# A half-rotary embedding on one core: where the first load is cut, when the second store is issued, and which queue carries the third

## The chip, the core and the metric

The kernel runs on one core of one Trainium2 chip. The metric is the device time of one execution in microseconds (us), as the median over several executions. The profile page belongs to one further execution taken with the hardware profiler; its span runs from the first to the last recorded instruction of the core.

## The reference

The input `x` is float32 with the shape (16, 512, 16, 64): batch, position, head, element. Only the first 32 elements of a head are rotated, the first 16 of them against the second 16, by the angle tables `cos` and `sin` of the position; the last 32 elements are passed through unchanged.

```python
x1, x2 = x[..., :32], x[..., 32:]
rotated_first  = x1[..., :16] * cos[..., :16] - x1[..., 16:] * sin[..., :16]
rotated_second = x1[..., :16] * sin[..., :16] + x1[..., 16:] * cos[..., :16]
return np.concatenate([rotated_first, rotated_second, x2], axis=-1)
```

All of `x` has to be read and all of the output written: 33.55 MB each way.

## The kernel before

The positions are cut into four tiles, t = 0 to 3. A tile puts 16 consecutive positions ("rows", `K = 16`) on each of the 128 partitions; a row is 16 heads of 64 elements, 4 KB, so that a tile is 64 KB per partition and 8.39 MB in all. Three tiles fit on the chip at a time: `ring` has three slots (`NS = 3`), and tile t lies in slot t mod 3. Tile 3 therefore goes into the slot of tile 0 and cannot be loaded before tile 0 has been stored.

Everything is done in place in the ring. `load(t, lo, hi)` (L55) brings rows lo to hi of a tile, `store(t)` (L58) sends a whole tile out, passed-through elements included. Both are issued from the SP queue, which issues in program order and stops at the first transfer whose condition does not yet hold. One transfer reads or writes one contiguous run per partition, 4 KB times its number of rows. Only the two small table loads (L63, L64, 64 KB each) go through GpSimd's queue (POOL).

VectorE (DVE) first clears a staging tile (L61), spreads the two tables over all partitions when they have arrived (L73, L80, L83), and then does the arithmetic. `rotate(t, lo, hi)` handles rows lo to hi with four instructions: L96 multiplies by the sine table into `b_t` (a single buffer in PSUM), L97 multiplies by the cosine table in place, and L98 and L101 subtract and add `b_t`. A tile is rotated in two halves of 8 rows (`KC = 8`), and `turn(t)` is the two halves and the store.

The order on SP is that of the program: load 0, load 1, the first half of load 2; store 0, which waits for the arithmetic of tile 0; the second half of load 2; load 3 in two pieces of 14 rows and 2 rows (`KL = 14`), which wait until store 0 has landed; then stores 1, 2 and 3. Store 1 carries one dependence written by hand: besides its arithmetic it waits until the piece of 14 rows of load 3 (`near`) has landed.

Of the kernel before, what the change touches and what calls it, by code (L numbers as in the profile page):

```python
# [1 line left out]

# [4 lines left out]


@with_exitstack
def kernel(  # L10
    ctx: ExitStack,
    tc: tile.TileContext,
    x: bass.AP,
    cos: bass.AP,
    sin: bass.AP,
    out: bass.AP,
):
    nc = tc.nc
    fp32 = mybir.dt.float32
    P = 128  # L20
    B, S, H, D = x.shape
    Q = D // 4
    HF = D // 2

    K = 16
    T = B * S // (P * K)
    PB = S // K
    REP = P // PB  # L30
    R = H * D
    NS = 3
    KC = K // 2
    KL = 14

    xf = x.rearrange("b s h d -> (b s h d)").rearrange("(t p f) -> t p f", t=T, p=P)
    of = out.rearrange("b s h d -> (b s h d)").rearrange("(t p f) -> t p f", t=T, p=P)
    cosf = cos.rearrange("(p k) j -> p (k j)", k=K)
    sinf = sin.rearrange("(p k) j -> p (k j)", k=K)

    const_pool = ctx.enter_context(tc.tile_pool(name="const", bufs=1))
    b_pool = ctx.enter_context(tc.tile_pool(name="bp", bufs=1, space=bass.MemoryType.PSUM))


    ring = const_pool.tile([P, NS, K, H, D], fp32)
    stage = const_pool.tile([P, 2, K, HF], fp32)
    spun = const_pool.tile([P, 2 * K, Q], fp32)
    packed = const_pool.tile([PB, 2 * K, Q], fp32)
    table = const_pool.tile([P, 2, K, 2, Q], fp32)

    def rows(t, lo, hi):
        return ring[:, t % NS, lo:hi].rearrange("p k h d -> p (k h d)")

    def load(t, lo=0, hi=K):
        return nc.sync.dma_start(out=rows(t, lo, hi), in_=xf[t, :, lo * R : hi * R])  # L55

    def store(t, lo=0, hi=K):
        return nc.sync.dma_start(out=of[t, :, lo * R : hi * R], in_=rows(t, lo, hi))  # L58


    nc.vector.memset(stage[:, :, :, 0:Q], 0.0)  # L61
    spread = stage.rearrange("(j b) t k i -> j b t (k i)", b=REP)
    nc.gpsimd.dma_start(out=spread[:, 0, 0], in_=cosf)  # L63
    nc.gpsimd.dma_start(out=spread[:, 0, 1], in_=sinf)  # L64
    load(0)
    load(1)
    load(2, 0, KC)

    PQ = PB // REP
    nc.vector.stream_shuffle(  # L73
        out=spun[:],
        in_=stage.rearrange("p t k j -> p (t k) j")[:, :, 0:Q],
        mask=[j % PQ * REP for j in range(PB)],
    )
    for q in reversed(range(REP)):
        n = PQ * (q + 1)
        nc.vector.tensor_copy(out=packed[0:n], in_=spun[q * PB : q * PB + n])  # L80

    for r in range(REP):
        nc.vector.tensor_copy(  # L83
            out=table[r * PB : (r + 1) * PB].rearrange("p t k c j -> p (t k) c j"),
            in_=packed.unsqueeze(2).to_broadcast((PB, 2 * K, 2, Q)),
        )
    C = table[:, 0].rearrange("p k c j -> p k (c j)")
    Sn = table[:, 1].rearrange("p k c j -> p k (c j)")

    def rotate(t, lo, hi):  # L90
        x1 = ring[:, t % NS, lo:hi, :, 0:HF]
        c = C[:, lo:hi].unsqueeze(2).to_broadcast((P, hi - lo, H, HF))
        s = Sn[:, lo:hi].unsqueeze(2).to_broadcast((P, hi - lo, H, HF))
        b_full = b_pool.tile([P, KC, H, HF], fp32, name="b_t")
        b_t = b_full[:, 0 : hi - lo]
        nc.vector.tensor_mul(out=b_t, in0=x1, in1=s)  # L96
        nc.vector.tensor_mul(out=x1, in0=x1, in1=c)  # L97
        nc.vector.tensor_sub(  # L98
            out=x1[:, :, :, 0:Q], in0=x1[:, :, :, 0:Q], in1=b_t[:, :, :, Q:HF]
        )  # L100
        nc.vector.tensor_add(  # L101
            out=x1[:, :, :, Q:HF], in0=x1[:, :, :, Q:HF], in1=b_t[:, :, :, 0:Q]
        )

    def turn(t):
        rotate(t, 0, KC)
        rotate(t, KC, K)
        return store(t)

    turn(0)  # L110
    load(2, KC, K)
    near = load(3, 0, KL)
    load(3, KL, K)

    tc.add_manual_dep(
        turn(1).ins,
        near.ins.name,
        mybir.DependencyInfo(mybir.DependencyClass.Sync, mybir.DependencyReason.DATA),
        reason="the store follows the loads at the DMA engines",
    )  # L120
    turn(2)
    turn(3)


# [1 line left out]
_INS = ['x', 'cos', 'sin']  # L126
_OUTS = [((16, 512, 16, 64), 'float32')]


# [23 lines left out]
```

## Time and profile before

| what | before |
|---|---|
| median of 8 executions | 161.54 us (161.46 to 161.68) |
| profiled execution, its own time | 161.5 us |
| profiled execution, span | 159.7 us |
| DVE busy | 112.4 us, 70% of the span |
| POOL busy | 1.4 us |
| moved by DMA | 67.24 MB, 421 GB/s over the span |

The profiled execution's own time is 1.8 us longer than its span, and it lies within 0.04 us of the median. A DMA is listed where it was issued; its "us to landing" is the time from there to the last of its bytes. Transfers issued by one queue land one after the other here, so the time between two landings says how long the later one took. The DMA share is that of the 16 DMA engines together; in short windows it can exceed 1 or fall to 0, because a packet is counted whole where it begins.

### The profile page before, as it was taken

Reading aid. Unit: us, or ns where it says so; the run is one execution under the profiler, and the core shown is the slowest. Engines: PE = TensorE matmul, PEld = TensorE weight load, DVE = VectorE, ACT = ScalarE, POOL = GpSimd, SP = SyncE. Lnnn points to the kernel's source line nnn. Section 1 sums busy time; section 2 is a strip of 40 time slices with the busy share of each in tenths; the row PEclk is TensorE's granted clock in tenths of the full one; section 3 lists DMA queues with packets and bytes.
Section 4 is the critical chain, followed back from the end, with each engine's and each line's share of the span. In section 5 each row is a group of like instructions: output and inputs, shape, how many; then the busy total and the mean of one; then the engine's idle time right before and its main releaser. Section 6 shows DMA issues by size and latency. Waiting matters only on the chain.

```text
span 159.7 us, 113 instructions
## 1 busy us (share of the span) xinstructions
DVE 112.4 (70%) x43; POOL 1.4 (1%) x6
## 2 busy tenths in 40 slices
DVE  1000959999999999999999999999999960000000
POOL 3000000000000000000000000000000000000000
DMA  7969989999799699699999995996996996996992
GB/s 263 542 263 542 427 361 525 394 394 525 304 476 533 295 492 525 279 377 451 468 460 460 460 460 244 544 525 263 525 525 263 525 525 263 525 509 279 525 427 98
DMA packets 1504, 67.24 MB, mean 421 GB/s; under 512 B 192, under 2 KB 192, under 8 KB 224
## 3 DMA queue, kind: packets, MB, share of 16 engines
q1 hardware_dynamic: 1440, 67.11, 97.7%
q0 software_dynamic: 64, 0.13, 0.2%
HBM read 33.69 MB, written 33.55 MB: 421 GB/s over the span
## 4 chain that ended last, share of the span: by engine, by line
DVE 59%; DMA 14%; issue 7%; DVEq 1%
DVE b_t L96 22%; DVE ring L97 22%; DMA ring<-in_x_dram 14%; DVE ring L101 10%; DVE ring L98 4%; DVEq L148 1%; DVEq L96 0%
## 5 line engine op out<-in xcount | busy, mean ns | idle before, releaser
L96 DVE TENSOR_TENSOR b_t<-ring,table 128x4096 f32<-128x4096 f32 x8 | 35.5, 4432 | 2.1 <-DMA ring<-in_x_dram 1.9
L97 DVE TENSOR_TENSOR ring<-ring,table 128x4096 f32<-128x4096 f32 x8 | 35.4, 4424 | 0.3
L98 DVE TENSOR_TENSOR ring<-ring,b_t 128x2048 f32<-128x2048 f32 x8 | 18.3, 2287 | 0.3
L101 DVE TENSOR_TENSOR ring<-ring,b_t 128x2048 f32<-128x2048 f32 x8 | 18.2, 2280 | 0.0
L73 DVE LOAD_MASK_SELECT spun<-stage x1 | 0.0, 14 | 14.4 <-DMA stage<-in_sin_dram 14.4
L83 DVE COPY table<-packed 32x1024 f32<-32x1024 f32 x4 | 2.7, 684 | 0.1
L80 DVE COPY packed<-spun 32x512 f32<-32x512 f32 (+3 forms) x4 | 1.7, 416 | 0.1
L61 DVE MEMSET stage<- 128x512 f32 x1 | 0.5, 485 | 0.9 <-PEq L137 0.9
L73 DVE STREAM_SHUFFLE spun<-stage 128x512 f32<-128x512 f32 x1 | 0.7, 723 | 0.0
L63 POOL DMA_DIRECT2D stage<-in_cos_dram x1 | 0.6, 649 | 1.3 <-DVE stage L61 1.3
L64 POOL DMA_DIRECT2D stage<-in_sin_dram x1 | 0.5, 532 | 0.0
L137 POOL MEMSET const-float32-0.0<- 128x1 f32 x1 | 0.1, 93 | 0.2 <-issue 0.2
L137 POOL MEMSET const-bfloat16-1.0<- 128x1 bf16 x1 | 0.1, 95 | 0.0
L137 POOL MEMSET const-float32-1.0<- 128x1 f32 x1 | 0.1, 93 | 0.0
L137 POOL MEMSET const-uint8-127<- 128x1 uint8 x1 | 0.1, 92 | 0.0
## 6 DMA issues: line engine op xcount, KB each, us to landing
ring<-in_x_dram SPq DMA_DIRECT2D x2, 4096.0 KB, 40.7
ring<-in_x_dram SPq DMA_DIRECT2D x1, 7168.0 KB, 26.6
ring<-in_x_dram SPq DMA_DIRECT2D x1, 1024.0 KB, 28.7
stage<-in_cos_dram POOLq DMA_DIRECT2D x1, 64.0 KB, 9.0
stage<-in_sin_dram POOLq DMA_DIRECT2D x1, 64.0 KB, 13.3
out_dram<-ring SPq DMA_DIRECT2D x4, 24.9
ring<-in_x_dram SPq DMA_DIRECT2D x2, 31.7
```

The lines of the kernel that those rows point to most:

```text
L61: nc.vector.memset(stage[:, :, :, 0:Q], 0.0)
L63: nc.gpsimd.dma_start(out=spread[:, 0, 0], in_=cosf)
L64: nc.gpsimd.dma_start(out=spread[:, 0, 1], in_=sinf)
L73: nc.vector.stream_shuffle(out=spun[:], in_=stage.rearrange("p t k j -> p (t k) j")[:, :, 0:Q], mask=[j % PQ * REP for j in range(PB)],)
L80: nc.vector.tensor_copy(out=packed[0:n], in_=spun[q * PB : q * PB + n])
L83: nc.vector.tensor_copy(out=table[r * PB : (r + 1) * PB].rearrange("p t k c j -> p (t k) c j"), in_=packed.unsqueeze(2).to_broadcast((PB, ...
L96: nc.vector.tensor_mul(out=b_t, in0=x1, in1=s)
L97: nc.vector.tensor_mul(out=x1, in0=x1, in1=c)
L98: nc.vector.tensor_sub(out=x1[:, :, :, 0:Q], in0=x1[:, :, :, 0:Q], in1=b_t[:, :, :, Q:HF])
L101: nc.vector.tensor_add(out=x1[:, :, :, Q:HF], in0=x1[:, :, :, Q:HF], in1=b_t[:, :, :, 0:Q])
L137: nc = _bacc.Bacc("TRN2", target_bir_lowering=False, num_devices=1)
L148: with _tile.TileContext(nc) as tc:
```

## The change

Four things are changed. Load 0 becomes two transfers of 4 and 12 rows. Load 3 becomes one transfer of 16 rows. The arithmetic of the second half of tile 2 is cut into 5 rows and 3 rows (`KM = 13`), and store 1 waits for the last instruction on the 5 rows instead of a landing of load 3. Store 2 is issued from GpSimd's queue instead of SP's. `turn` is written out in full; `rotate` returns its last instruction so that store 1 can name it.

```diff
-    KL = 14
+    KM = 13
...
-    def store(t, lo=0, hi=K):
-        return nc.sync.dma_start(out=of[t, :, lo * R : hi * R], in_=rows(t, lo, hi))
+    def store(t, lo=0, hi=K, queue=nc.sync):
+        return queue.dma_start(out=of[t, :, lo * R : hi * R], in_=rows(t, lo, hi))
...
-    load(0)
+    load(0, 0, KC // 2)
+    load(0, KC // 2, K)
     load(1)
     load(2, 0, KC)
...
-        nc.vector.tensor_add(
+        return nc.vector.tensor_add(
             out=x1[:, :, :, Q:HF], in0=x1[:, :, :, Q:HF], in1=b_t[:, :, :, 0:Q]
         )
...
-    def turn(t):
-        rotate(t, 0, KC)
-        rotate(t, KC, K)
-        return store(t)
-
-    turn(0)
+    rotate(0, 0, KC)
+    rotate(0, KC, K)
+    store(0)
     load(2, KC, K)
-    near = load(3, 0, KL)
-    load(3, KL, K)
+    load(3)
+    rotate(1, 0, KC)
+    rotate(1, KC, K)
+    behind_loads = store(1)
+    rotate(2, 0, KC)
+    near = rotate(2, KC, KM)
+    rotate(2, KM, K)
+    store(2, queue=nc.gpsimd)
 
     tc.add_manual_dep(
-        turn(1).ins,
+        behind_loads.ins,
         near.ins.name,
         mybir.DependencyInfo(mybir.DependencyClass.Sync, mybir.DependencyReason.DATA),
         reason="the store follows the loads at the DMA engines",
     )
-    turn(2)
-    turn(3)
+    rotate(3, 0, KC)
+    rotate(3, KC, K)
+    store(3)
```

## The prediction

> **What bounds the kernel now.** I read the page first: how busy the engines are, and what the DMA queues moved.
>
> ```profile
> DVE 112.4 (70%) x43; POOL 1.4 (1%) x6
> ...
> q1 hardware_dynamic: 1440, 67.11, 97.7%
> q0 software_dynamic: 64, 0.13, 0.2%
> HBM read 33.69 MB, written 33.55 MB: 421 GB/s over the span
> ```
>
> No compute engine is near full. The packets of q1 (the SP queue) hold the 16 DMA engines 97.7% of the span, so the first suspicion is that the kernel is a pipe that is already full. Section 4 of the page seems to say otherwise, with DVE on 59% of the chain that ended last. In order of time, that chain ends so:
>
> ```profile
> 121.61 4.43 DVE ring L97
> 126.05 0.02 issue
> 126.07 2.29 DVE ring L98
> 128.36 2.20 DVEq L148
> ```
>
> It stops at 130.56, 29 us before the end of the span, and leaves out the last two stores. So I rebuilt the landings by hand from the trace, one answer per window around each issue: issue time plus "us to landing". The SP lines of the timeline give the issues, these two the end of it:
>
> ```profile
> 98.38 0.34 SPq L58 DMA_DIRECT2D out_dram<-ring  x1
> ...
> 103.69 0.34 SPq L58 DMA_DIRECT2D out_dram<-ring  x1
> ...
> 130.58 0.33 SPq L58 DMA_DIRECT2D out_dram<-ring  x1
> ```
>
> Load 0 lands at 22.9, load 1 at 42.3, half of load 2 at 52.0, store 0 at 71.7, the other half at 81.4, load 3 at 98.3 and 100.8, store 1 at 98.38 + 21.7 = 120.1, store 2 at 103.69 + 35.7 = 139.4, store 3 at 130.58 + 28.1 = 158.7. A tile takes 19.3 us in every one of these steps (8.39 MB / 19.3 us = 435 GB/s), whether load or store, with two exceptions: load 0 needs 22.2 us from its issue, and store 0 19.7. Each transfer is issued before its forerunner has landed: stores 0, 1, 2, 3 by 2.1, 2.4, 16.4 and 8.8 us. DVE, too, is kept waiting by data only at the start:
>
> ```profile
> DVE spun L73 <- DMA stage<-in_sin_dram: 14.4, 1, 14.4
> DVE b_t L96 <- DMA ring<-in_x_dram: 1.9, 1, 1.9
> ```
>
> Eight tiles' worth at 19.3 us are 154.4 us of the 159.7. Of the remaining 5.3, load 0 holds 22.2 - 19.3 = 2.9, its issue at 0.74, the teardown after the last landing 1.0, store 0 some 0.4, small change the rest. **The DMA engines are the bound from about 2 us to 158.7 us**, and an edit counts only if it changes the bytes, opens a hole in that stream, or changes the rate.
>
> **What the Trainium skill says.** (1) "DMA: Bandwidth & Descriptors", section "Issuing engines are not separate DMA queues": transfers from SP and GpSimd run on the same 16 DMA engines and interleave. The trace agrees: the tables on q0 land at 10.7 and 15.7, among SP's packets, though 64 KB each. (2) The same page, "SWDGE vs HWDGE vs iDMA": on GpSimd's queue software writes the descriptors, and packets are preferably at most 4096 B. The DMA summary counts 32 packets between 2 and 8 KB, which for 0.13 MB is 4 KB each: two 2 KB rows put together. Whether a 64 KB row stays whole there, the trace before does not show. (3) "SBUF — State Buffer", "Who interferes with whom": `tensor_tensor` has no 2-port mode; with both inputs in SBUF it contends with GpSimd's reads only, and that descriptor writing escapes it is called inferred. Not shown here either: POOL issues at 1.70 and 2.35, when DVE is idle. (4) "VectorE: DVE Perf Modes", "The TRN2 errata", gives (N + 151) / 0.96 ns for an fp32 `tensor_tensor`: 4424 ns for 4096 elements, and L97's row has 4424. I use its slope below.
>
> **The change part by part.**
>
> *Load 0 in two.* One more SP issue, 0.42 us (median of L55's first three), ahead of load 1. Covered: load 0's bytes keep the engines busy to 22.9, and load 1 is then issued near 1.6 instead of 1.2. Each partition has one more run here and one fewer in load 3 (joined into one), ten transfers of 128 runs before and after: the per-run and per-completion costs cancel. The join also makes SP issue once at 71.7 instead of twice (0.81 us for both): hidden, as the second half of load 2 fills the engines to 81.4. DVE does not start earlier: rows 0 to 8 touch both pieces, so L96 still waits for the second to land, near 22.9. The shorter first runs let the table packets of q0 in sooner, so `sin` may land some us before 15.7; table work (15.81 to 21.18) then ends earlier, but already ended 1.9 us before load 0. Worth nothing. What I can't price is the slow start: of the 2.9 us extra, about 1.0 is from issue to the first packet (DMA is first busy near 1.7), 0.3 the tables' bytes (q0 has 1.3% of the first 25 us), the rest the first fill and the completion. Shorter first runs could save half of that 1.6, or cost a little: -0.8 to +0.2; I take 0, since a first fill is a wait for the first bytes, which the length of the run does not shorten.
>
> *DVE, tile 2's second half in 5 and 3 rows.* Eight rows are 12,288 elements in four instructions and step 13.44 us (76.81 to 90.25), of which 12,288 / 0.96 = 12.80 us streams and 0.64 is fixed. Five rows: 8.00 + 0.64 = 8.64; three rows: 4.80 + 0.64 = 5.44. So `near` ends at 90.25 + 8.64 = 98.9, tile 2 at 104.3 instead of 103.7, tile 3 at 131.2 instead of 130.6. The cost is 0.64 us on DVE, hidden: the engines hold stores 1 and 2 until 139.4, so store 3 at 131.2 still comes 8.2 us early. With that cover gone it would cost 0.64.
>
> *Store 1 at a point of DVE's work.* Issue moves from 98.4 to 98.9; the loads end at 100.8, so its lead shrinks from 2.4 to 1.9 us. Store 0 had 2.1, and the engines were 100.3% busy from 50 to 58, across that handover; its 0.4 us lie elsewhere. So 0, at worst 0.4. Behind it on SP waits only store 3, not due before 131.2. A late `near` would delay nothing else.
>
> *Store 2 through POOL.* A POOL issue costs 0.65 us (L63) beside SP's 0.34, at 104.3; POOL has nothing else, and SP loses a transfer and its wait. From about 106 two queues share the engines: if turn about, store 1 lands near 134 instead of 120 and store 2 near 144, and then store 3 runs alone to the same end, since the sum of bytes stays. No slot waits for those landings (there is no further load). From 4.5 to 16 us, with packets of both queues mixed, the engines were busy throughout (q1 105.1%, q0 2.9%); a change of queue shows no price. Bounds: if 64 KB rows stay whole, 0; if they are cut to 4 KB, the dearest that the trace suggests, the second rival. A gain has no room: the rate is 435 GB/s already. I take 0.
>
> *Sum:* 0 + 0 + 0 + 0 = 161.5 us for the profiled execution (159.7 of span and 1.8 around it), 0.04 below the median of the runs; so 161.54. A measurement of this kernel can tell some 0.2%, 0.32 us, from no change.
>
> **The rivals.**
>
> *A gain at the start.* Half of the 1.6 us of slow start goes: 160.8; a quarter: 161.1. For it: load 0 is the only step that is far from 19.3. Against it: the stream needs one first fill in any case. Chance 0.14.
>
> *Slower: POOL's rows travel in small packets.* Store 2 cut into 4 KB packets gives each of 16 engines 128 of them. From 7 to 8 us q0's 16 packets hold 15.9% of 16 engines, 159 ns each, where 4096 B at 435 / 16 = 27.2 GB/s take 151: 8 ns lost on each, or half of that where neighbours overlap. So 19.3 us becomes 19.8 to 20.3, and all of it is on the path, as the engines never rest: 162.0 to 162.5. It decides as soon as a packet's overhead exceeds 2.5 ns (128 x 2.5 = 0.32 us). For it: the 4 KB packets on q0. Against: those are two short rows joined, not a long one cut. Imperfect sharing of two store streams at HBM would look and cost alike. Chance 0.22.
>
> *Slower: DVE keeps POOL from writing descriptors.* Then store 2 starts when tile 3's arithmetic ends. SP's stream is dry at 120.1; from there to 131.2 plus about 1 us to the first byte the engines idle, and two tiles (38.6) follow: 12 us more, 173.6. It decides if the descriptors come later than 119; a lock during L96 and L97 alone, until 113.2, costs nothing. Against it: the skill's section above. Chance 0.03.
>
> *The change does nothing measurable*, the forecast: 0.61.
>
> **How the numbers follow.** Within 0.2%: 0.61, own range 161.25 to 161.85. Faster: 0.14. Slower: 0.22 + 0.03 = 0.25. The range leaves out the 12 us case, the deeper half of the gain and the dearest packets: 161.0 to 162.4.
>
> **What would show it.** Right: q1 and q0 together busy as now, q0 with 8.5 MB in 64 KB packets; store 1 issued at 98.9, landing past 130; store 2 on POOL at 104.3; store 3 issued at 131.2 and landing at 158.7; DVE busy 0.6 us longer. Small packets: a q0 of thousands of packets, and store 3's landing 0.5 to 1 us later. A lock: store 2's first packets only after 113 or 131, empty DMA slices near 120 to 131. A gain at the start: L96 begins before 22.7. The forecast is wrong if the last landing moves by over 0.3 us.

## The result and the profile after

The changed kernel takes 162.82 us in the median of 12 executions (161.45 to 163.54), the kernel before 161.55 in 32 (161.35 to 161.82). A thirteenth execution of the changed kernel, 164.33 us, is counted as slow, being more than 1.5% above its fastest, and may be the same loss once more; the median is 162.82 with it too. The ratio is 1.0072, 95% interval 1.0058 to 1.0086: slower, by more than the 0.2% that can be told, where no change was forecast. The scatter is news too: the kernel before stays within 0.5 us here, the changed one covers 2.1. Its profiled execution took 162.81 us, with a span of 160.6, so it is a typical one. Of its 1.3 us over the profiled execution of before, 0.9 lie in the span and 0.4 outside it, where the profile shows nothing; the experiments come back to the 0.4.

The lines of the page that answer to those shown of before:

```profile
DVE 112.9 (70%) x47; POOL 1.9 (1%) x7
...
q1 hardware_dynamic: 1296, 58.72, 85.2%
q0 software_dynamic: 208, 8.52, 12.3%
HBM read 33.69 MB, written 33.55 MB: 419 GB/s over the span
```

Store 2 has moved from q1 to q0, 8.4 MB of it. The packets together are still 97.5% of the span, and the page counts 1504 of them as before, so nothing was cut into small pieces. DVE has 0.5 us more and waits for data only at the start:

```profile
DVE spun L74 <- DMA stage<-in_sin_dram: 8.6, 1, 8.6
DVE b_t L97 <- DMA ring<-in_x_dram: 7.7, 1, 7.7
```

The tables arrive 5.9 us sooner, and DVE then waits that much longer for load 0: its arithmetic starts at 23.02, as before. The chain in order of time ends at 131.2 (before: 130.6) and again leaves out the last stores:

```profile
126.67 0.03 issue
126.70 2.29 DVE ring L99
128.99 2.20 DVEq L153
```

The DMA issues of the timeline, SP's and POOL's, after 90 us:

```profile
98.88 0.34 SPq L58 DMA_DIRECT2D out_dram<-ring  x1
...
104.60 0.56 POOL L58 DMA_DIRECT2D out_dram<-ring  x1 [101.73 <-DVE ring L102]
...
131.21 0.34 SPq L58 DMA_DIRECT2D out_dram<-ring  x1
```

With their times to landing, store 1 lands at 98.88 + 34.2 = 133.1, store 2 at 104.60 + 40.5 = 145.1, store 3 at 131.21 + 28.4 = 159.6. That last landing was at 158.7 before: the 0.9 us that the span has grown. The question is where the stream of transfers lost them. Two answers of the trace, the second half of load 2 (L55, issued at 50.3) before and after, show it. First before:

```profile
L55 SPq DMA_DIRECT2D ring<-in_x_dram x1: 432/432/432, 50.3 to 50.3; - x1
...
DMA to landing us min/median/max: 31.1/31.1/31.1
```

And after:

```profile
L55 SPq DMA_DIRECT2D ring<-in_x_dram x1: 433/433/433, 50.3 to 50.3; - x1
...
DMA to landing us min/median/max: 32.0/32.0/32.0
```

Store 0, just ahead of it, lands at 71.6 (71.7 before); the load behind it lands at 82.3 instead of 81.4. **The whole 0.9 us is lost by 82 us**, before store 1, store 2 or the joined load 3 have moved a byte. It is not lost by all 16 engines alike. Between 81.5 and 82.4 us the kernel before starts no packet at all: all engines are inside their first 56 KB run of load 3 (a run is the contiguous piece of one partition, and makes one packet).

```profile
DMA packets 0, 0.00 MB, mean 0 GB/s; under 512 B 0, under 2 KB 0, under 8 KB 0
```

After:

```profile
DMA packets 4, 0.13 MB, mean 146 GB/s; under 512 B 2, under 2 KB 2, under 8 KB 2
```

Two completions (packets of 4 bytes, one behind the last run of each engine in a transfer) and two 64 KB runs: two engines come to load 3 this late. The packet records (start, length and size of each packet) do not name the engine, but an engine that does not wait begins its next packet within 0.01 us of the end of its last one, so that they can be strung into 16 chains. Each chain moves about 4.2 MB in the whole execution, so nobody takes work off a late engine. The two reach load 3 at 81.6 and 82.0, the others by 81.2; at the end two finish at 158.9 and 159.3, the others by 158.4. A transfer lands with its latest engine.

A 64 KB packet takes 2.418 us here; I add what an engine's packets take beyond their size, and the gaps between them. Around store 0 there are two handovers, load 2 to store 0 near 51 us and store 0 to load 2 near 70 us:

| lost per engine, us | load to store | store to load, mean | store to load, worst engine |
|---|---|---|---|
| before | 0.00 | 0.48 | 1.03 |
| after | 0.02 | 0.72 | 1.85 |

In both kernels most of the loss at 70 us sits in the last run of the store, which takes up to 3.44 us before and 3.36 after instead of 2.418. After, two engines also begin store 0's first run late, by 0.28 us together, the second at 51.31, 1.41 us after that store's issue. No engine of the kernel before waits there.

### The profile page after: what moved, and what is told of

It reads as the page before. It is cut to its first block, busy times and chain, and to the rows that moved or that the text cites. A ratio compares the mean times of both kernels' runs of the same rounds, so it can differ in the third digit from the quotient of the medians.

```text
span 160.6 us, 116 instructions
## 1 busy us (share of the span) xinstructions
DVE 112.9 (70%) x47; POOL 1.9 (1%) x7
## 2 busy tenths in 40 slices
DMA packets 1504, 67.24 MB, mean 419 GB/s; under 512 B 192, under 2 KB 192, under 8 KB 224
## 4 chain that ended last, share of the span: by engine, by line
DVE 61%; DMA 14%; issue 5%; DVEq 1%; SPq 0%
DVE b_t L97 22%; DVE ring L98 22%; DMA ring<-in_x_dram 14%; DVE ring L102 10%; DVE ring L99 7%; DVEq L153 1%; SPq L55 0%; DVEq L97 0%
## 5 line engine op out<-in xcount | busy, mean ns | idle before, releaser
L97 DVE TENSOR_TENSOR b_t<-ring,table 128x4096 f32<-128x4096 f32 (+2 forms) x9 | 35.6, 3959 | 8.0 <-DMA ring<-in_x_dram 7.7
L98 DVE TENSOR_TENSOR ring<-ring,table 128x4096 f32<-128x4096 f32 (+2 forms) x9 | 35.5, 3950 | 0.3
L99 DVE TENSOR_TENSOR ring<-ring,b_t 128x2048 f32<-128x2048 f32 (+2 forms) x9 | 18.4, 2049 | 0.3
L102 DVE TENSOR_TENSOR ring<-ring,b_t 128x2048 f32<-128x2048 f32 (+2 forms) x9 | 18.4, 2042 | 0.0
L58 POOL DMA_DIRECT2D out_dram<-ring x1 | 0.6, 559 | 101.7 <-DVE ring L102 101.7
## 6 DMA issues: line engine op xcount, KB each, us to landing
ring<-in_x_dram SPq DMA_DIRECT2D x1, 6144.0 KB, 21.7
out_dram<-ring SPq DMA_DIRECT2D x3, 28.4
out_dram<-ring POOLq DMA_DIRECT2D x1, 40.5
```

The source lines that it names most:

```text
L58: return queue.dma_start(out=of[t, :, lo * R : hi * R], in_=rows(t, lo, hi))
L99: nc.vector.tensor_sub(out=x1[:, :, :, 0:Q], in0=x1[:, :, :, 0:Q], in1=b_t[:, :, :, Q:HF])
L102: return nc.vector.tensor_add(out=x1[:, :, :, Q:HF], in0=x1[:, :, :, Q:HF], in1=b_t[:, :, :, 0:Q])
```

## The experiments

The kernels of one table ran on one chip with the kernel before (the fourth table's last two on another); different tables ran on different chips. In the recorded expectations "most runs" are executions, while a "first run" is the contiguous piece of a transfer.

**First: one edit at a time.**

*Split only.*

```diff
-    load(0)
+    load(0, 0, KC // 2)
+    load(0, KC // 2, K)
```

> The kernel before with one edit: load 0 as 4 and 12 rows. In the profile of the changed kernel one DMA engine begins the second half of load 2 about 1.1 us late, near 71 us, and stays late to the end. Only the split of load 0 comes ahead of that point. Theory H (the handover from store 0 to load 2, disturbed by what the split does to the start): this kernel shows the whole loss, 162.5 to 163.0 us with a wide scatter. Theory Q (two queues): no change, 161.5 to 161.7. Theory J (load 3 as one transfer, issued at 71.7 in the middle of that handover): no change, 161.5 to 161.7.

*Store 2 on POOL only.*

```diff
-    turn(2)
+    rotate(2, 0, KC)
+    rotate(2, KC, K)
+    store(2, queue=nc.gpsimd)
```

> The kernel before with one edit: store 2 issued from GpSimd's queue. Theory Q (two queues that share the engines cost time or put one engine behind): 162.3 to 163.0 us. Theories H and J: no change, 161.4 to 161.8, as in the profile of the changed kernel the stretch with both queues shows no packet slower than 2.43 us.

*Joined load 3 and the point of DVE's work only*: the changed kernel with `load(0)` and `store(2)`.

> The kernel before with two edits that belong together: load 3 as one transfer, and store 1 released by DVE's 5-row point of tile 2. Load 0 is whole and store 2 is on SP's queue. Theory J: 162.3 to 163.0 us, with one engine late from 71 us on. Theories H and Q: no change, 161.5 to 161.8; DVE ends 0.64 us later, hidden.

*All but POOL.*

```diff
-    store(2, queue=nc.gpsimd)
+    store(2)
```

> The changed kernel with store 2 back on SP's queue. Theory Q: back to 161.5 to 161.8. Theories H and J: still 162.5 to 163.0, as nothing ahead of 104 us is different from the changed kernel.

| kernel | median (range), us | ratio to before, 95% |
|---|---|---|
| split only | 161.67 (161.35 to 163.01), 22 executions | 1.0028 (1.0010 to 1.0045) |
| store 2 on POOL only | 161.66 (161.46 to 162.24), 13 executions | 1.0002 (0.9991 to 1.0013) |
| join and point only | 161.59 (161.32 to 161.94), 13 executions | 1.0002 (0.9994 to 1.0010) |
| all but POOL | 162.78 (161.34 to 163.75), 22 executions | 1.0053 (1.0033 to 1.0074) |

Theories Q and J fall: by themselves their edits do not change the time. Theory H stands with a correction: the split alone gives two groups of times, 8 of 22 executions at 162.6 to 163.0 and 11 at 161.35 to 161.6, so the loss comes in some executions and not in others. With the join and the point beside it 12 of 22 lie at 162.7 or above, one more at 162.56; 8 against 13 of 22 is too near to say that those edits add to it. All but POOL and join and point differ in the split alone, and ran on one chip: 162.78 against 161.59. The profile of all but POOL (163.75 us) repeats the picture of after, stronger: its second half of load 2 lands at 50.19 + 32.7 = 82.9. From 81.5 to 83 us:

```profile
DMA packets 10, 0.46 MB, mean 306 GB/s; under 512 B 3, under 2 KB 3, under 8 KB 3
```

Again a few engines are late, and at 51 us four engines had begun store 0's first run late, by 0.59 us together. Some 0.5 us more is lost by the last engine at the handover from load 3 to store 1, near 100 us. The profile of split only fell on a quick execution (161.38) and has no such wait.

The 0.4 us outside the span belong here too. In the medians of all executions the time outside is 1.8 us in the kernel before, with the split only and with POOL only, and 1.9 to 2.1 in every kernel that has the join and the point. With join and point only a shorter span makes up for it (159.6 us against 159.8). The runs show no cause for either.

**Second: what in the split, and is it needed?**

*Load 1 in 4 and 12 rows instead of load 0, in the kernel before*: `load(1, 0, KC // 2)`, `load(1, KC // 2, K)`.

> The kernel before with load 1, not load 0, as 4 and 12 rows. Theory N (number: four loads instead of three are queued on SP ahead of store 0, and every later transfer has another place in the queue): two groups of times as with the split of load 0 alone, about a third of the runs near 162.8 us and the rest near 161.5. Theory S (start: the short first runs and the early table packets set the engines into another step): one group, 161.4 to 161.9 us, as before.

*Load 0 in 8 and 8, in the kernel before*: `load(0, 0, KC)`, `load(0, KC, K)`.

> The kernel before with load 0 as 8 and 8 rows. Theory N: a third or more of the runs near 162.8 us. Theory S: fewer runs or none near 162.8, since the first runs are twice as long and the tables land later than with 4 and 12.

*Changed kernel, tile 2 cut at 10 rows.*

```diff
-    load(2, 0, KC)
+    load(2, 0, 10)
...
-    load(2, KC, K)
+    load(2, 10, K)
```

> The changed kernel with the loads of tile 2 cut at 10 rows instead of 8, so that store 0 is issued some 4.5 us instead of 2.1 us ahead of its turn. Theory L (lead: store 0 comes so late that some engines wait up to 0.43 us for it at 51 us, and the late ones stay late): back to 161.4 to 161.8 us. Theories N and S: still most runs near 162.8.

*Changed kernel, load 0 whole.*

```diff
-    load(0, 0, KC // 2)
-    load(0, KC // 2, K)
+    load(0)
```

> The changed kernel with load 0 whole again, all else as changed. If the split is the whole cause: 161.4 to 161.8 us in one group. If GpSimd's queue or the joined load 3 takes part by itself: above 162.

| kernel | median (range), us | ratio to before, 95% |
|---|---|---|
| load 1 in 4 and 12 | 161.60 (161.45 to 162.95), 22 executions | 1.0011 (1.0000 to 1.0021) |
| load 0 in 8 and 8 | 162.61 (162.60 to 162.65), 5 executions | 1.0062 (1.0050 to 1.0074) |
| changed, cut at 10 rows | 162.59 (162.45 to 162.79), 5 executions | 1.0060 (1.0048 to 1.0072) |
| changed, load 0 whole | 161.60 (161.28 to 161.79), 13 executions | 0.9997 (0.9989 to 1.0005) |

The last row, with the pair on one chip in the first table, settles the cause among the edits: **take the split out, keep the other three, and the loss and the scatter are gone.** Its second half of load 2 is back at 50.3 + 31.1 (its two lines are those shown of before, word for word), and store 0 at 49.9 + 21.7.

With load 1 in two, 2 of 22 executions take 162.55 and 162.95 us and 2 more 162.1; the kernel before itself reached 162.3 twice in the 114 executions on two of the chips. So long executions are not wholly tied to the split of load 0, only far more frequent with it. Theory N had expected a third of them.

The 8-and-8 and the 10-row kernel missed in an instructive way: slower by 1 us, but with hardly any scatter in their five executions each. In both, store 0 is queued far ahead of its turn. With 10 rows that was meant; with 8 and 8 it came unasked, since DVE can begin on rows 0 to 8 when the first piece is there and issues store 0 at 44.17 instead of 49.9. The SP lines of the 10-row kernel, store 0:

```profile
L58 SPq DMA_DIRECT2D out_dram<-ring x1: 348/348/348, 49.7 to 49.7; - x1
...
DMA to landing us min/median/max: 25.5/25.5/25.5
```

It lands at 75.2; two rows more ahead of it are 2.4 us, so 73.9 to 74.1 was to be expected. By the packet records the engines lose 1.3 us on the mean, and each at least 1.0, at the handover from load to store (8 and 8: 1.2 us near 50) and nothing at the one from store to load. Here it is the last two runs of the load that take longer: again the transfer that goes out. So theory L is false: in both kernels with a store that comes this early all engines lose.

**Third: move store 0 by fractions of a microsecond.** Its margin, from issue to the mean moment at which an engine has finished load 2's first half, is 1.37 us before and 1.31 after. (The 2.1 us of the prediction ran to the landing, which comes after the last engine.)

*Changed and before, 0.5 us earlier*: `rotate(0, KC, K, skip=2)`, where `skip` starts the rows of the last addition (L102 of the changed kernel) later. Both kernels leave out two rows of that addition.

> The changed kernel with store 0 issued about 0.53 us earlier: the last add on the second half of tile 0 leaves out 2 of 8 rows (512 elements less). Theory M (margin: after the split the engines come to store 0's turn some 0.1 us sooner, while its issue stays at 49.9; the runs of one or more engines are then not there yet, and those engines are set back again at the handover to load 2): back to 161.4 to 161.7 us, in one group. Theory S (the split sets the engines into another step, whatever the margin): still most runs near 162.8.

> The kernel before, load 0 whole, with store 0 issued about 0.53 us earlier (2 of 8 rows of the same add left out). Theory M: 161.4 to 161.7 us, as the margin was enough; if instead the rule of the 10-row and the 8-and-8-row kernels already holds here (a store queued well ahead costs all engines some 1.2 us at 49 to 55 us, and nothing at 70), 162.4 to 162.7. Theory S: 161.5 to 161.6.

*Before and changed, later.*

```diff
     rotate(0, 0, KC)
+    nc.vector.memset(spun[:, 0:16], 0.0)
     rotate(0, KC, K)
```

> The kernel before, load 0 whole, with store 0 issued about 0.3 us later: one clearing of 256 elements of a dead tile on DVE within the arithmetic of tile 0. Theory M: the loss appears without any split, many runs or all at 162.5 to 163.5 us, with engines that wait at 51 us. Theory S: 161.4 to 161.8, or at most the 0.3 us of the later issue.

> The changed kernel with the same clearing, store 0 about 0.3 us later. Theory M: worse than the changed kernel, 163 us or more in nearly every run, with more engines waiting at 51 us. Theory S: as the changed kernel, near 162.8.

| kernel | median (range), us | ratio to before, 95% |
|---|---|---|
| changed, store 0 earlier | 161.45 (161.29 to 161.80), 13 executions | 0.9995 (0.9987 to 1.0003) |
| before, store 0 earlier | 161.39 (161.26 to 161.60), 13 executions | 0.9989 (0.9981 to 0.9998) |
| before, store 0 later by 0.2 | 161.67 (161.50 to 161.90), 13 executions | 1.0009 (1.0001 to 1.0017) |
| changed, store 0 later | 162.15 (161.40 to 163.40), 21 executions | 1.0050 (1.0031 to 1.0068) |

**Half a microsecond of margin takes the whole loss out of the changed kernel**, the split still in it, though a little arithmetic is left out. Its landings of store 0 and of the load behind it are 49.3 + 22.4 = 71.7 and 49.7 + 31.4 = 81.1:

```profile
L55 SPq DMA_DIRECT2D ring<-in_x_dram x1: 434/434/434, 49.7 to 49.7; - x1
...
DMA to landing us min/median/max: 31.4/31.4/31.4
```

The first lands where it did, the second 1.2 us earlier than in the changed kernel.

The two "later" kernels missed their purpose: the clearing depends on nothing in tile 0 and was put ahead of it, into DVE's wait for load 0, as the chain of instructions shows for the kernel with two of them further below. Store 0 was issued at 50.12 in the one and 49.79 in the other profile, as load 0 happened to land, not by the clearing. So they count as repeats of the kernel before and of the changed kernel, the latter on the chip of its cure (1.0050 against 0.9995), and the half of theory M that says a shorter margin alone brings the loss was not tested. One profile bears on it by chance: the kernel before with its store at 50.12 had a margin of 1.14 us and lost 0.66 us per engine at the next handover, 1.1 on the worst, and took 161.86 us. What is shown is that in the changed kernel **the loss needs both**: taking away either the split (0.9997) or the short margin (0.9995) ends it.

**Fourth: the margin without leaving work out, and the size of the first piece.**

*Tile 2 cut at 9 rows, in the kernel before and in the changed kernel*: `load(2, 0, 9)`, `load(2, 9, K)`.

> The kernel before with tile 2's loads cut at 9 rows instead of 8, so that store 0, issued at 49.9 as before, comes 1.2 us further ahead of its turn (some 2.6 us on the mean instead of 1.4); nothing is left out. From the two kernels with store 0 some 0.5 us earlier: the handover at 66 to 74 us costs 0.1 instead of 0.5 us, 161.2 to 161.4 us. If the loss of the 10-row cut (1.3 us at 49 to 56 us) begins below 2.6 us: 162.2 to 162.6.

> The changed kernel with the same cut at 9 rows. Theory M: one group, 161.2 to 161.5 us. If the margin only worked through the omitted arithmetic: still near 162.8 in most runs. If 2.6 us is already too early: near 162.5 in every run.

*Changed kernel, load 0 in 7 and 9, and in 2 and 14.*

> The changed kernel with load 0 as 7 and 9 rows; the arithmetic still waits for both pieces. Same number of transfers, first runs of 28 KB instead of 16 KB. Theory N (number of loads queued ahead of store 0): as the changed kernel, half or more of the runs at 162.4 to 163.5. Theory S (short first runs): fewer runs there, a quarter at most.

> The changed kernel with load 0 as 2 and 14 rows, first runs of 8 KB. Theory N: as the changed kernel. Theory S: at least as many runs at 162.4 to 163.5 as with 4 and 12.

*Before, 9 rows, store 0 later*: two `nc.vector.memset(spun[:], 0.0)` between the halves of tile 0.

> The kernel before with tile 2's loads cut at 9 rows and, within tile 0's arithmetic, two clearings of a dead tile (about 0.97 us), so that store 0 comes some 2.0 us ahead of its turn instead of 3.0; nothing is left out. If the cost of the two handovers around store 0 has its lowest point near 2 us (0.1 to 0.2 us at 1.9 and 2.0 us, 0.5 at 1.4, 0.4 at 3.0): 161.3 to 161.5 us, about 0.1 us under the kernel before. If only an earlier end of the arithmetic helps: 161.5 to 161.6.

*Changed kernel, tables on SP between the two pieces of load 0.*

```diff
-    nc.gpsimd.dma_start(out=spread[:, 0, 0], in_=cosf)
-    nc.gpsimd.dma_start(out=spread[:, 0, 1], in_=sinf)
     load(0, 0, KC // 2)
+    nc.sync.dma_start(out=spread[:, 0, 0], in_=cosf)
+    nc.sync.dma_start(out=spread[:, 0, 1], in_=sinf)
     load(0, KC // 2, K)
```

> The changed kernel with the two table loads on SP's queue between the two pieces of load 0, so that no packets of GpSimd's queue come in between the first runs. Theory T (the table packets, which with pieces of 4 and 7 rows fall into the first piece and with 2 rows after most of it, set single engines back at the start): the loss is gone, 161.4 to 161.7 us in one group. If they have no part in it: most runs still at 162.4 to 163.5.

| kernel | median (range), us | ratio to before, 95% |
|---|---|---|
| before, 9 rows | 161.56 (161.35 to 161.68), 13 executions | 0.9997 (0.9989 to 1.0005) |
| changed, 9 rows | 161.85 (161.54 to 162.27), 20 executions | 1.0018 (1.0012 to 1.0025) |
| changed, 7 and 9 | 162.96 (161.91 to 164.13), 18 executions | 1.0091 (1.0068 to 1.0114) |
| changed, 2 and 14 | 161.58 (161.31 to 161.68), 13 executions | 1.0000 (0.9992 to 1.0008) |
| before, 9 rows, later | 161.69 (161.47 to 161.82), 21 executions | 1.0010 (1.0004 to 1.0017) |
| changed, tables on SP | 162.99 (161.42 to 163.61), 7 executions | 1.0086 (1.0055 to 1.0118) |

The 9-row cut takes most of the loss out of the changed kernel, 1.0018 where it had 1.0072, with nothing left out; its median span is 159.8 us, that of the kernel before, and the rest lies outside the span. It does not make the kernel before faster. At a margin of 3.0 us the store-to-load handover costs 0.14 us on the mean and the load-to-store handover 0.15 in the kernel before (0.04 and 0.30 in the changed one); another 0.19 (0.09) is lost at 42 to 47 us, in load 2's runs of 36 KB and before store 0 is issued, so that it is not the price of an early store. The expectation of "before, 9 rows, later" counts it in (0.4 at 3.0). Together these take back what the store-to-load handover wins. The lowest point near 2 us that I then looked for ("before, 9 rows, later") was not tested, for the reason given above: the timeline has the clearing (the second of the two, L112) at 22.13, ahead of the arithmetic.

```profile
22.13 0.48 DVE L112 MEMSET spun<- 128x512 f32 x1 [0.17 <-DVE spun L111]
23.10 4.43 DVE L96 TENSOR_TENSOR b_t<-ring,table 128x4096 f32<-128x4096 f32 x1 [0.48 <-DMA ring<-in_x_dram]
```

Store 0 left at 49.98 instead of 49.82, and 161.69 us is the 9-row kernel once more, on another chip; its time outside the span is 1.9 us instead of 1.8, as in the other kernel before with a clearing. The fastest kernel of all, the one before with store 0 half a microsecond earlier (0.9989), leaves out work and is at the edge of what can be told; no complete version here beats the kernel before.

On the split itself three explanations fell. It is not the number of transfers alone (theory N): 2 and 14 has the same number as 4 and 12 and no loss, on the chip on which 7 and 9 has a larger one. It is not that the first runs are short (theory S): the shortest are the harmless ones. It is not the table packets of GpSimd's queue (theory T): with the tables on SP the loss stays, and five engines begin store 0's first run late, by 0.81 us together. The order over 2, 4 and 7 rows suggests, and no more, that the size of the first piece matters; the 16-row load is harmless again. One sign goes with the loss wherever a profile caught it: in all five profiles of split kernels above 162.5 us with tile 2 cut at 8 rows and load 0 in 2 to 7 rows first (after, all but POOL, changed with the clearing, 7 and 9, tables on SP) one to five engines wait near 51 us for store 0's first run, 0.12 to 0.81 us together, and in the quick profiles, split or whole, none waits more than 0.02 us. The wait and the loss do not grow together: with 0.12 us of waits (changed with the clearing) and with 0.81 (tables on SP) the load behind store 0 lands at 82.4 alike. Nor does a wait cost much by itself: in the changed kernel with 9 rows nine engines wait for store 1's first run near 100 us, 1.0 us together, with another store behind it, and the last store lands at 158.79, where that of the kernel before with 9 rows lands at 158.78. How the first piece, 30 us earlier, brings engines and runs out of step, and why a wait at 51 us is followed by a loss of 1 to 2 us at the next handover, **stays open**.

## Why the prediction was wrong

By its own steps:

- *What bounds the kernel*: right. The engines are full, and an edit counts only by a hole in the stream. The hole is on single engines, which the shares of the page, means over 16, cannot show.
- *Load 0 in two, taken as 0 from a range of -0.8 to +0.2*: **the step that failed.** It is worth +1.2 us in the company of the other edits (162.82 against 161.60 with load 0 whole, on different chips; 162.78 against 161.59 on one chip, with store 2 on SP). The term was sized in the wrong place: I looked for its effect at the start, where it is small (0.61 us lost per engine at the first fill against 0.65, so that part held), and not at the next tight place downstream. That load 0 would still land near 22.9, and the tables earlier for nothing, was right: DVE began at 23.02.
- *Store 0*: the prediction saw it take 19.7 us instead of 19.3, wrote "0.4 us lie elsewhere", and went on. That 0.4 to 0.5 was the store-to-load handover, the one place after the start where the engines of the kernel before lose more than a few hundredths of a us. It named store 1's margin as the thing to watch, and store 0's, of the same size, as the proof that such a margin is safe.
- *DVE in 5 and 3 rows*: right to 0.1 us (98.88, 104.33, end at 131.2), hidden as said.
- *Store 1 at a point of DVE's work, joined load 3*: right in the time, 1.0002, but the margin of store 1 is used up: in the profile of join and point only, three engines wait for its first run (0.1 us together), and nine in the changed kernel with 9 rows.
- *The sum*: the 1.8 us around the span were carried over; they measured 2.2 in the profiled execution. The kernel with load 0 whole has the same growth and a shorter span (159.5 in the median), so the verdict does not hang on it.
- *Store 2 through POOL*: right, 1.0002 alone and 0.9997 with the joined load and the point. The trace decides what the prediction had to bound. Between 107 and 133 us the two queues take turns, run by run, and q0 has 96 packets with 6.29 MB, that is 64 KB rows left whole (of q1's 96, 16 are completions):

```profile
q0 software_dynamic: 96, 6.29, 55.8%
q1 hardware_dynamic: 96, 5.24, 46.5%
```

- *The rivals*: small packets, no (above). DVE keeping POOL from its descriptors until 113 or 131 us, no: store 2's instruction took 0.56 us at 104.60, within L97, its packets begin at 109.62, within L98, and its landing at 145.1 was put near 144. Those 5.0 us from issue to first packet compare with 3.9 us for the tables (1.70 to 5.62), with DVE idle; engines inside runs of 2.4 us can account for the difference, and a wait of about 1 us behind L97 is not excluded. So far this agrees with what "Who interferes with whom" in the Trainium skill's "SBUF — State Buffer" infers, that a `tensor_tensor` with both inputs in SBUF leaves descriptor writing free. A gain at the start, no: the quick executions of split only are 161.35 to 161.6. The chance of 0.25 for slower was given to two other mechanisms; the one that came was on no list: an edit that costs nothing where it stands and unsettles a margin 30 us later.

## What to carry to other kernels

When a queue is the bound, ask of each transfer how long before its turn it is issued, not only whether it is in time. Here one store between two loads, 1.4 us ahead, cost 0.5 us per engine, 2 us ahead 0.1 to 0.2, 3 us ahead 0.3 and 4 to 7 us ahead 1.2 to 1.3; and at 1.4 a change at the start was enough to put single engines behind for good. It was measured on this one store only. A share of 97% is a mean over 16 engines, while a transfer lands with its latest one: look at landings, one by one, before an edit is costed at nothing, and at the scatter between executions after it.

## What the runs showed of the hardware

- Between a load, a store and a load behind them the handovers have a price that moves with the store's margin. With store 0 queued early (3.9 and 7 us ahead of the turn that the bytes alone give) load to store costs 1.2 to 1.3 us per engine on the mean and store to load nothing; with 1.4 us it is 0 and 0.5 us; with 1.9 and 2.0 us, 0 and 0.1 to 0.2; with 3.0 us, 0.15 to 0.3 and 0.04 to 0.14. Most of it is in the last one or two runs of the transfer that goes out.
- The first run of a store reached an engine as late as 1.65 us after its issue (all but POOL), where the first engine of the kernel before had it without a wait 1.0 us after the issue.
- An engine that falls behind does not catch up: the changed kernel has two late ones at 82 us, 0.45 and 0.85 us behind the last of the others, and at the end two that are behind by the same; each engine moves about 4.2 MB of the 67.
- Two queues that store side by side cost nothing measurable (1.0002, 0.9991 to 1.0013), and share the engines packet by packet in turn (from 107 us on, 16 runs of one queue, then 16 of the other).
- From GpSimd's queue the first packet came 3.9 us after the issue with VectorE idle (the tables of the changed kernel) and 5.0 us after it in the middle of the arithmetic.
